# Other bounds and a place in the order for the triangular inverse of a hybrid decoder trunk

## The chip, the cores and the metric

The kernel runs on 1 core of one Trainium2 chip. The metric is device time in microseconds. An interval or a verdict compares runs of two kernels on the same chip.

## The reference

One layer on 1024 positions of width 1024, all in float32. After an RMS norm one projection feeds four groups of heads, whose outputs are normalised per head, gated and projected back:

```python
(aq, ak, av, ag, bq, bk, bv, bg, cq, ck, cv, cg, cf, d_in, dg) = _split(rms_norm(x, norm_gain) @ w_in, IN_WIDTHS)
oa = differential_attention(...)    # A: 4 heads, two softmaxes each, subtracted
ob = stick_breaking_attention(...)  # B: 8 heads, cumulative products, no softmax
oc = forgetting_attention(...)      # C: 8 heads, softmax with a forget bias
od = rwkv7_branch(...)              # D: 8 heads, a recurrence over the positions
mixed = concatenate([oa * silu(ag), ob * silu(bg), oc * silu(cg), od * silu(dg)])
return x + mixed @ w_out
```

The recurrence of group D is, for each head and position,

```python
sa = einsum('bhij,bhj->bhi', state, -kk_t)
state = state * w_t + sa[..., None] * b_t + v_t[..., None] * k_t
y_t = einsum('bhij,bhj->bhi', state, r_t)
```

## The kernel before, in words

Group D is computed in 16 chunks of 64 positions. Within a chunk the recurrence is a unit lower triangular system of 64 x 64; with 16 chunks and 8 heads there are 128 of them, one per SBUF partition. `inv_steps` inverts all of them at once on POOL (GpSimd): step r multiplies column r below the diagonal by row r (L855, `ytmp`) and adds the product to the rows below (L857, `yinv`), with 63 - r rows of r elements, cut into pieces of at most 512 elements. Steps 1 to 62 make 106 pairs of POOL instructions, each needing the one before. `inv_load` brings the matrices, `inv_store` (L861) writes the inverses to the DRAM tile `abky`, from which group D's chunks read them when all attention is done.

The attention runs as twelve jobs in a row, four of group B, four of A, four of C (the loop over `jobs`). A job projects q, k, v for its heads (`proj`, L280: 48 matmuls of 128x512 per projection, with each weight tile in two parts, `wh` in the matmul's own format and `wl` the rest), then runs `scores` (L397, L401), the group's own function of the scores, transposes of the result (L417) and the product with v (L426 to L431). The projections of job i + 1 and some gates are written behind the attention of job i, and fill TensorE between its scores. `load_w` loads half a projection's weights (`raw`, on SP's queue, L186) and has POOL split them: `wh` (L191) and `wl` (L192), two buffers each. So POOL serves the projections; in group B it also sets single columns of the scan (L472, L474), in group A it scales one softmax's exponentials (L565) ahead of the difference on DVE (L568), in group C it makes the bias tile (L613, L614) from a row `cb` that SP loads, and scales (L617). The pool that holds `yinv` and `ytmp` is closed after job 7, A3, and the pool with `cb` takes its memory.

The order of the instructions on each engine is set when the kernel is built, by a scheduler that takes, among the instructions that are ready by its own estimate, the one of the lowest priority number; each engine then runs its queue strictly in that order. The inverse is written behind each of the first eight jobs, in eight parts given by `INV_BOUNDS`, and `later(LATER)` adds 5000 to its priority number, so it goes wherever POOL would otherwise be free. `after(inst, first)` adds a dependency that the scheduler keeps in its order and that puts no semaphore into the program.

Of the kernel before, what the change touches and what calls it, by code (L numbers as in the profile page):

```python
# [19 lines left out]
P = 128  # L20
# [15 lines left out]
           dlo=7688, dg=7752)  # L36
C_ID, C_BLK, C_MS, C_MC, C_MR, C_MK, C_MN, C_I2, C_END = 0, 128, 256, 384, 512, 640, 768, 832, 896
NB = 32
INV_BOUNDS = [0, 8, 14, 20, 26, 32, 40, 50, 64]
LATER = 5000  # L40
NPT = 12
SB = 1
# [48 lines left out]
def hybrid_trunk_kernel(  # L91
# [23 lines left out]
    nc = tc.nc  # L115
# [3 lines left out]
    def pool(stack, name, bufs=1, space=None, side="left"):  # L119
        kw = {"side": side, "reuse_waits": "tile"} if space is None else {"space": space}  # L120
        return stack.enter_context(tc.tile_pool(name=name, bufs=bufs, **kw))
# [26 lines left out]
    def after(inst, first):  # L148
        tc.add_manual_dep(inst.ins, first.name if isinstance(first, mybir.InstLoadActFuncSet) else first.ins.name, mybir.DependencyInfo(
            mybir.DependencyClass.NoSync, mybir.DependencyReason.DATA), reason="order")  # L150
# [11 lines left out]

    exp_ln_tables()

# [1 line left out]
    cst = cp.tile([P, C_END], F32, name="cst")  # L166
    def vec(src, n, name, eng=nc.sync):
        t = cp.tile([P, n], F32, name=name)
# [61 lines left out]
    nc.vector.tensor_scalar(qkg[:, 0:1], qkg[:, 0:1], 0.125, None, op0=ALU.mult)  # L230
    nc.vector.tensor_scalar(qkg[:, 2:3], qkg[:, 2:3], 0.125, None, op0=ALU.mult)

# [1 line left out]
    hTh = hpool.tile([P, KT, S], F32R, name="hTh")  # L234
    hTl = hpool.tile([P, KT, S], F32R, name="hTl")

# [6 lines left out]
    with xst:  # L243
# [14 lines left out]
        for hf in range(2):  # L258
            for kt in range(KT):
# [5 lines left out]
                split = nc.scalar.activation(dh, ps, AF.Copy, scale=ng[:, kt:kt + 1])  # L265
# [1 line left out]
                    after(split, norms[ACTORD[kt]])  # L267
                nc.vector.scalar_tensor_tensor(dl, ps, ng[:, kt:kt + 1], dh.bitcast(F32), op0=ALU.mult, op1=ALU.subtract)  # L268

# [1 line left out]
    def proj(col, evac, M=P, hold=None, wts=None):  # L271
        wts = load_w(col) if wts is None else wts
        pss = [bank("pj", 2, "pj") for _ in range(2)]
        for hf in range(2):
            cs = slice(hf * HS, (hf + 1) * HS)
            n = 0
            for kt in range(KT):
                wh, wl = wts[kt // 4]
                for a, b in ((wh, hTh), (wh, hTl), (wl, hTh)):
                    mm = nc.tensor.matmul(pss[hf][:M, :], lhsT=a[:, kt % 4, :M], rhs=b[:, kt, cs], start=n == 0, stop=n == 3 * KT - 1)  # L280
                    if n == 0 and hold is not None:
                        after(mm, hold)
                    n += 1
            evac(hf, cs, pss[hf])

# [1 line left out]
    class Att:  # L287
        pass

    at = Att()  # L290
# [79 lines left out]
    def proj_gate(f, tmp):  # L370
        def evac(hf, cs, ps):
            e = tmp.tile([P, HS], F32, tag="pjt", bufs=2, name="ge")
            sigmoid(e, ps)
            nc.vector.tensor_mul(e, ps, e)
            nc.sync.dma_start(gates[f, :, cs], e)

        proj(COL["abcd"[f // 4] + "g"] + f % 4 * P, evac)
# [68 lines left out]
        nc.gpsimd.tensor_mul(y, y, gt)  # L446
        nc.sync.dma_start(mix[f * P:f * P + P, cs], y)

# [1 line left out]
    def proj_pair_b(p, pl, tmp):  # L450
        t = qk_tiles(pl)
        proj_qk(COL["bq"] + p * P, "q", t, None, tmp)
        proj_qk(COL["bk"] + p * P, "k", t, None, tmp)
        t["v"] = proj_v(COL["bv"] + p * P, pl, tmp, 2)
        return t
# [40 lines left out]
        else:  # L496
            finish(ot, f, J, blk, 64, tmp)

# [1 line left out]
    def setup_a(tmp):  # L500
        oht = tmp.tile([NB, OHW], F32, tag="oh", bufs=1, name="oht")
        nc.sync.dma_start(oht, onehot)
# [76 lines left out]
            else:  # L579
                finish(ot, p, J, ones, 128, tmp)  # L580

# [1 line left out]
    at.fbt = cp.tile([72, 1], F32, name="fbt")  # L583
    after(nc.sync.dma_start(at.fbt[64:72, :], forget_bias.rearrange("o h -> h o")), w_dma[-1])
    at.fb = at.fbt[64:72]
# [45 lines left out]
            else:  # L631
                finish(ot, 8 + p, J, blk, 64, tmp)

# [1 line left out]
    rw = Att()  # L635

    def spill(name):
# [201 lines left out]
                nc.scalar.copy(dst[64 * h:64 * h + 64, :, c2, :], src[64 * c2:64 * c2 + 64, :, h, :])  # L839
        keep(rw.rkv, 2, vt)  # L840

# [1 line left out]
    def inv_load(ip):  # L843
        rw.y = ip.tile([P, CH, CH], F32, name="yinv")
        rw.ytmp = ip.tile([P, 512], F32, name="ytmp")
        nc.sync.dma_start(rw.y.rearrange("p a b -> p (a b)"), rw.mab.rearrange("p c h t s -> (p c h) (t s)"))

    def inv_steps(r0, r1):
        y = rw.y
        for r in range(max(r0, 1), min(r1, CH - 1)):  # L850
            step = max(1, 512 // r)
            for a in range(r + 1, CH, step):
                n = min(step, CH - a)
                t = rw.ytmp[:, :n * r].rearrange("p (a b) -> p a b", b=r)
                nc.gpsimd.tensor_mul(t, y[:, a:a + n, r:r + 1].to_broadcast([P, n, r]),  # L855
                                     y[:, r:r + 1, :r].to_broadcast([P, n, r]))
                nc.gpsimd.tensor_add(y[:, a:a + n, :r], y[:, a:a + n, :r], t)  # L857

    def inv_store():
        for q in range(4):  # L860
            nc.sync.dma_start(rw.abky[:, :, 3, q].rearrange("c (h t) s -> (c h) t s", h=2), rw.y[32 * q:32 * q + 32])  # L861

# [1 line left out]
    def split_w(f, opr, wh, wl):  # L864
        raw = opr.tile([P, DM], F32, tag="raw", bufs=2, name="wraw")
        nc.sync.dma_start(raw, w_out[0, f * P:(f + 1) * P, :])
        eng = nc.vector if f in WDVE else nc.gpsimd
        if len(wh) == 1:
            nc.scalar.copy(wh[0], raw)
            eng.tensor_sub(wl[0], raw, wh[0].bitcast(F32))  # L870
        else:
            for h in range(2):
                cs = slice(h * HS, (h + 1) * HS)
                nc.scalar.copy(wh[h], raw[:, cs])
                eng.tensor_sub(wl[h], raw[:, cs], wh[h].bitcast(F32))
# [185 lines left out]
            op(y3, y3, b)  # L1061
        nc.sync.dma_start(mix[12 * P:16 * P, ts_].rearrange("(q p) t -> p q t", p=P), y3)

# [1 line left out]
    with ExitStack() as st:  # L1065
        dp0 = pool(st, "dp0", 1)
        dp = pool(st, "dp", 1)
# [12 lines left out]
    with ExitStack() as st:  # L1080
        pl = pool(st, "attw", 1)
        late_pools = st.enter_context(ExitStack())
        pp = pool(late_pools, "attp", 1)
        tmp = pool(late_pools, "attt", 1)
        side = late_pools.enter_context(ExitStack())
        inv_load(pool(side, "ip", 1))
        bounds = INV_BOUNDS
        nxt = None
        for i, (pf, af, j) in enumerate(jobs):
            cur = pf(j, pl, tmp) if nxt is None else nxt  # L1090
            at.first = None
            af(j, cur, pl, pp, tmp)
            if i == 7:
                side.close()
                at.cbp = pool(side, "cbp", 1)
            if i == 3:
                late = []
                nxt = proj_head_a(0, pl, tmp, late)
                for f in FILL[i]:
                    proj_gate(f, tmp)  # L1100
                table = exp_ln_tables()
                for g in late:
                    g(table)
            else:
                nxt = jobs[i + 1][0](jobs[i + 1][2], pl, tmp) if i + 1 < len(jobs) else None
            if i < 3:
                for f in FILL[i]:
                    proj_gate(f, tmp)
                gate_d(i, tmp)
                if i == 2:  # L1110
                    gate_d(3, tmp)
            elif i >= 7:
                for f in FILL[i]:
                    proj_gate_exp(f, at.first if i in HOLD else None)
            for f in FIN.get(i, []):
                for J in range(2):
                    finish_later(f, J, tmp)
            if i + 1 < len(bounds):
                with later(LATER):
                    inv_steps(bounds[i], bounds[i + 1])  # L1120
                    if i + 2 == len(bounds):
                        inv_store()

        hp.close()
        opr = pool(st, "opr", 1, side="right")
        rp = pool(st, "rp", 1, side="right")
        rwkv_chain_setup(rp)
        yts = {}

        def chain(c0, c1):  # L1130
            for c in range(c0, c1):
                if c % 2 == 0:
                    yts[0] = rp.tile([P, 4, P], F32, tag="yt", bufs=2, name="yt")
                chunk_state(c, rp, yts[0], chunk_local(c + 1, rp) if c + 1 < NCH else iter(()))
                if c % 2:
                    rwkv_norm(c // 2, yts[0], rp)

        for _ in chunk_local(0, rp):
            pass
        wo = {}  # L1140
        chain(0, CUT1)
        split_w_early(pl, opr, wo)
        pair = out_blocks(0, 2, wo)
        for _ in range(EARLYG):
            next(pair)
        chain(CUT1, CUT2)
        for h in at.held:
            finish(*h)
        for f in LASTF:
            for J in range(2):  # L1150
                finish_later(f, J, tmp)
        late_pools.close()
        op = pool(st, "op", 1)
        if WFIRST:
            split_w_late(op, opr, wo)
        chain(CUT2, NCH)
        if not WFIRST:
            split_w_late(op, opr, wo)
        for _ in pair:
            pass  # L1160
        for tb in range(2, 8):
            for _ in out_blocks(tb, 1, wo):
                pass
# [29 lines left out]
```

## Time and profile before

| What | Value |
|---|---|
| median of 3 runs | 1626.15 us (1625.5 to 1627.73) |
| span of the profiled execution | 1628.0 us, 23497 instructions; no other time is listed for it |
| PE (TensorE matmul) busy | 1555.1 us, 96% |
| DVE (VectorE) busy | 978.7 us, 60% |
| ACT (ScalarE) busy | 744.3 us, 46% |
| POOL (GpSimd) busy | 906.2 us, 56% |
| the inverse: L855 and L857 | 106 each, 120.6 and 127.3 us |

Shares are means over stages with different limits, so the trace is read in windows. Busy PE counts overlapping matmuls once; what the clock costs does not show in it, and stands in the column of the granted clock. Idle time counts where the engine in question sets the end. "x <- y" means that x waited for y.

### The profile page before, as it was taken

The numbers are of one execution on the slowest core, as the hardware profiler recorded it, in microseconds if no ns is written. First come the engines' busy times: TensorE is split into PE (matmuls) and PEld (weight loads), VectorE is DVE, ScalarE is ACT, GpSimd is POOL, SyncE is SP. The second block draws the span as 40 slices with busy tenths as digits, with TensorE's granted clock in tenths as the row PEclk, the third lists the DMA queues.
The fourth block names the chain that finished last, engine by engine and source line by source line (L and its number), as shares of the span: only waits on it lengthen the run. The fifth ranks groups of instructions, "written<-read, shape, count | busy, mean of one in ns | idle before, by whom it ended". The sixth has DMA issues, their size and how long they took to land.

```text
span 1628.0 us, 23497 instructions
## 1 busy us (share of the span) xinstructions
PE 1555.1 (96%) x8180; PEld 1183.9 (73%) x8180; DVE 978.7 (60%) x1739; ACT 744.3 (46%) x1601; POOL 906.2 (56%) x992
## 2 busy tenths in 40 slices
PE   6899999999989899899999999999999999999999
PEld 4777777767667676576777777777777678788887
DVE  6677763776998888466556544453456774544321
ACT  5534433443444445545556555565566654311110
POOL 3566755999999998133323356757576744300000
PEclk9999999999999999999999999999999999999999
DMA  6454567212222222622322233323227456755232
GB/s 159 102 132 102 132 163 200 59 43 71 56 62 56 78 78 57 170 52 59 98 71 72 78 91 111 97 79 111 84 84 187 120 135 165 210 140 130 82 104 65
DMA packets 259758, 168.76 MB, mean 104 GB/s; under 512 B 127948, under 2 KB 222412, under 8 KB 259512
## 3 DMA queue, kind: packets, MB, share of 16 engines
q1 hardware_dynamic: 259640, 167.26, 39.1%
q8 instruction: 65, 1.06, 0.3%
q14 instruction: 53, 0.43, 0.1%
HBM read 107.40 MB, written 49.60 MB: 96 GB/s over the span
## 4 chain that ended last, share of the span: by engine, by line
PE 64%; POOL 16%; DVE 7%; issue 6%; ACT 3%; DMA 3%; SPq 1%; POOLq 0%; DVEq 0%; ACTq 0%
PE pj L280 27%; PE pso L931 10%; POOL yinv L857 5%; POOL ytmp L855 5%; PE sc L401 5%; PE psf L968 4%; PE pt L417 3%; PE sc L397 3%; PE psn L295 3%; POOL wl L192 2%; PE po L427 2%; PE po L426 1%; POOL wh L191 1%; DMA wraw<-in_w_out_dram 1%; POOL sh L682 1%
## 5 line engine op out<-in xcount | busy, mean ns | idle before, releaser
L280 PE MATMUL pj<-hTh,wh 128*128 128x512 f32 (+1 forms) x1040 | 424.8, 409 | 14.6 <-POOL wh L191 7.2
L280 PE MATMUL pj<-hTh,wl 128*128 128x512 f32 (+1 forms) x1040 | 419.0, 407 | 12.5 <-POOL wl L192 12.1
L280 PE MATMUL pj<-hTl,wh 128*128 128x512 f32 (+1 forms) x1040 | 415.8, 400 | 0.3 <-DVE hTl L268 0.3
L280 PEld LDWEIGHTS pj<-hTh,wh 128*128 128x128 f32 (+1 forms) x1040 | 198.2, 191 | 69.7 <-issue 17.9
L280 PEld LDWEIGHTS pj<-hTh,wl 128*128 128x128 f32 (+1 forms) x1040 | 197.8, 190 | 66.6 <-POOL wl L192 17.0
L280 PEld LDWEIGHTS pj<-hTl,wh 128*128 128x128 f32 (+1 forms) x1040 | 198.0, 190 | 44.0 <-issue 5.4
L192 POOL TENSOR_TENSOR wl<-raw,wh 128x512 fp32r<-128x512 f32 (+1 forms) x130 | 185.5, 1427 | 10.5 <-PE pj L280 4.9
L191 POOL TENSOR_SCALAR wh<-raw 128x512 fp32r<-128x512 f32 (+1 forms) x130 | 100.0, 769 | 155.5 <-PE pj L280 137.7
L421 DVE TENSOR_TENSOR ptl<-pt,pth 128x512 fp32r<-128x512 f32 x240 | 126.4, 549 | 68.0 <-ACT pth L420 67.5
L420 ACT CAST pth<-pt 128x512 fp32r<-128x512 f32 x240 | 109.0, 481 | 126.8 <-PE pt L417 107.5
L475 DVE TENSOR_TENSOR_SCAN qs<-qs 128x128 f32<-128x128 f32 (+3 forms) x96 | 136.6, 1429 | 11.3 <-ACT qs L138 11.3
L553 ACT ACTIVATE Pt<-Pt,st 128x512 f32<-128x512 f32 (+2 forms) x192 | 116.8, 611 | 53.5 <-DVE st L548 52.7
L857 POOL TENSOR_TENSOR yinv<-yinv,ytmp 128x486 f32<-128x486 f32 (+44 forms) x106 | 127.3, 1201 | 4.0
L401 PE MATMUL sc<-k,ql 64*128 64x512 f32 (+3 forms) x288 | 127.6, 443 | 0.0
L855 POOL TENSOR_TENSOR ytmp<-yinv 128x486 f32<-128x486 f32 (+44 forms) x106 | 120.6, 1137 | 8.4 <-DMA raw<-in_w_in_dram 4.3
L477 DVE TENSOR_TENSOR Pt<-Pt,qs 128x128 f32<-128x128 f32 (+3 forms) x96 | 102.3, 1072 | 35.0 <-POOL qs L474 19.1
L417 PE MATMUL pt<-cst,Pt 128*128 128x128 f32 x720 | 118.0, 276 | 3.8 <-DVE Pt L477 3.8
L397 PE MATMUL sc<-k,q 128*128 128x512 f32 (+3 forms) x288 | 116.1, 403 | 2.1 <-DVE st L548 1.1
L1061 POOL TENSOR_TENSOR yc<-yc,lbg 128x512 f32<-128x512 f32 x16 | 21.2, 1325 | 150.7 <-DVE yc L1055 150.3
L417 PEld LDWEIGHTS pt<-cst,Pt 128*128 128x128 f32 x720 | 86.5, 141 | 23.3 <-issue 5.6
L401 PEld LDWEIGHTS sc<-k,ql 64*128 64x128 f32 x288 | 53.1, 185 | 68.0 <-issue 61.3
L613 POOL TENSOR_SCALAR bt<-cb,cumq 128x128 f32<-128x128 f32 (+3 forms) x64 | 52.9, 828 | 70.3 <-DVE st L548 67.8
(254 smaller groups left out, 2961.4 us busy)
## 6 DMA issues: line engine op xcount, KB each, us to landing
raw<-in_w_in_dram SPq DMA_DIRECT2D x128, 256.0 KB, 3.0
cb<-cum SPq DMA_DIRECT2D x16, 512.0 KB, 4.0
bd<-abky SPq DMA_DIRECT2D x32, 256.0 KB, 5.7
wraw<-in_w_out_dram SPq DMA_DIRECT2D x16, 512.0 KB, 4.0
om<-mix SPq DMA_DIRECT2D x32, 256.0 KB, 3.1
q<-q SPq DMA_DIRECT2D x48, 128.0 KB, 2.2
k<-kl SPq DMA_DIRECT2D x48, 128.0 KB, 2.3
gl<-gates SPq DMA_DIRECT2D x24, 256.0 KB, 3.0
```

What stands on the lines that cost most here:

```text
L191: nc.gpsimd.tensor_scalar(wh[:, :, :M], raw[:, :, :M], 1.0, 0.0, op0=ALU.mult, op1=ALU.add)
L192: nc.gpsimd.tensor_sub(wl[:, :, :M], raw[:, :, :M], wh[:, :, :M].bitcast(F32))
L280: mm = nc.tensor.matmul(pss[hf][:M, :], lhsT=a[:, kt % 4, :M], rhs=b[:, kt, cs], start=n == 0, stop=n == 3 * KT - 1)
L397: mm = nc.tensor.matmul(ps[:, :w], lhsT=t[f"q{h}"][qh][:, qs], rhs=t[f"k{h}"][:, c0:c1], start=True, stop=False)
L401: nc.tensor.matmul(ps[:, :w], lhsT=t["ql"][qh][n:n + 64, qs], rhs=t[f"k{h}"][n:n + 64, c0:c1], start=False, stop=not diag)
L417: nc.tensor.transpose(pt[:, (b - a) * P:(b - a + 1) * P], ptiles[b][kb // 4][:, kb % 4 * P:(kb % 4 + 1) * P], ident)
L421: nc.vector.tensor_sub(pl[:, :n], pt[:, :n], ph[:, :n].bitcast(F32))
L475: nc.vector.tensor_tensor_scan(q[:, :w][:, ::-1], q[:, :w][:, ::-1], q[:, :w][:, ::-1], 1.0 if after is None else after, op0=ALU.mult, op1 ...
L553: nc.scalar.activation(et[:, :w], et[:, :w], AF.Exp, scale=-1.0, bias=init, accum_out=st[:, 2 + i:3 + i])
L855: nc.gpsimd.tensor_mul(t, y[:, a:a + n, r:r + 1].to_broadcast([P, n, r]), y[:, r:r + 1, :r].to_broadcast([P, n, r]))
L857: nc.gpsimd.tensor_add(y[:, a:a + n, :r], y[:, a:a + n, :r], t)
L931: mm = nc.tensor.matmul(ps[b][half], lhsT=l, rhs=r[half], start=n == 0, stop=n == 47)
```

## The change

`INV_BOUNDS` moves the cuts: the parts written behind B0 to B3 now hold r = 1 to 11, 12 to 16, 17 to 21, 22 to 26, and those behind A0 to A3 r = 27 to 34, 35 to 41, 42 to 50, 51 to 62. Each multiplication of a part is placed behind `at.first`, the first score matmul of the job it is written behind.

```diff
-INV_BOUNDS = [0, 8, 14, 20, 26, 32, 40, 50, 64]
+INV_BOUNDS = [0, 12, 17, 22, 27, 35, 42, 51, 64]
...
-    def inv_steps(r0, r1):
+    def inv_steps(r0, r1, hold):
...
-                nc.gpsimd.tensor_mul(t, y[:, a:a + n, r:r + 1].to_broadcast([P, n, r]),
-                                     y[:, r:r + 1, :r].to_broadcast([P, n, r]))
+                mul = nc.gpsimd.tensor_mul(t, y[:, a:a + n, r:r + 1].to_broadcast([P, n, r]),
+                                           y[:, r:r + 1, :r].to_broadcast([P, n, r]))
+                after(mul, hold)
                 nc.gpsimd.tensor_add(y[:, a:a + n, :r], y[:, a:a + n, :r], t)
...
-                    inv_steps(bounds[i], bounds[i + 1])
+                    inv_steps(bounds[i], bounds[i + 1], at.first)
```

The rest of the diff turns comment lines into empty ones. The added line moves the addition from L857 to L858 and the store from L861 to L862.

The scheduler makes new orders of all engines from this. Three places show it; a row is one instruction, output tile, inputs, shape.

First, POOL in job B0, at the 45th and 46th pair of weight halves, before:

```order
L191 TENSOR_SCALAR wh<-raw 128x512
L472 MEMSET qs 128x1
L855 TENSOR_TENSOR ytmp<-yinv 128x240
L192 TENSOR_TENSOR wl<-raw,wh 128x512
L857 TENSOR_TENSOR yinv<-yinv,ytmp 128x15x16
L191 TENSOR_SCALAR wh<-raw 128x512
L855 TENSOR_TENSOR ytmp<-yinv 128x510
L192 TENSOR_TENSOR wl<-raw,wh 128x512
L474 COPY qs<-qs 128x1
L857 TENSOR_TENSOR yinv<-yinv,ytmp 128x30x17
```

The same two pairs in the change:

```order
L191 TENSOR_SCALAR wh<-raw 128x512
L192 TENSOR_TENSOR wl<-raw,wh 128x512
L472 MEMSET qs 128x1
L474 COPY qs<-qs 128x1
L191 TENSOR_SCALAR wh<-raw 128x512
L192 TENSOR_TENSOR wl<-raw,wh 128x512
L472 MEMSET qs 128x1
```

The first part (r up to 11) is done by then, and the second waits for B1, so no step of the inverse stands between the halves here. Of the 36 gaps between pairs that held steps before, from the 38th pair to the 74th, 17 hold some now.

Second, POOL in job A0, at the 80th to 82nd pair, before:

```order
L191 TENSOR_SCALAR wh<-raw 128x512
L192 TENSOR_TENSOR wl<-raw,wh 128x512
L565 TENSOR_SCALAR Pt<-Pt,st 128x512
L565 TENSOR_SCALAR Pt<-Pt,st 128x384
L191 TENSOR_SCALAR wh<-raw 128x512
```

The same place in the change:

```order
L191 TENSOR_SCALAR wh<-raw 128x512
L855 TENSOR_TENSOR ytmp<-yinv 128x495
L192 TENSOR_TENSOR wl<-raw,wh 128x512
L858 TENSOR_TENSOR yinv<-yinv,ytmp 128x15x33
L565 TENSOR_SCALAR Pt<-Pt,st 128x512 x2
L855 TENSOR_TENSOR ytmp<-yinv 128x495
L191 TENSOR_SCALAR wh<-raw 128x512
L858 TENSOR_TENSOR yinv<-yinv,ytmp 128x15x33
L192 TENSOR_TENSOR wl<-raw,wh 128x512
L855 TENSOR_TENSOR ytmp<-yinv 128x510
L858 TENSOR_TENSOR yinv<-yinv,ytmp 128x15x34
L565 TENSOR_SCALAR Pt<-Pt,st 128x128
```

Steps stand between the halves and between the scalings, through all four A jobs; the last one comes between the 96th and the 97th pair, ahead of the first `bt` of C0.

Third, SP's queue of transfers around the store, between B3 and A0 before:

```order
L186 DMA raw<-in_w_in_dram 128x4x128
L861 DMA abky<-yinv 2048x1x64 x4
L375 DMA gates<-ge 128x512
L186 DMA raw<-in_w_in_dram 128x4x128
L535 DMA tb<-skew 128x1024 x2
L342 DMA ql<-late_qk 128x512
```

In the change the store stands between A3 and C0:

```order
L493 DMA otl<-otb 128x512
L862 DMA abky<-yinv 2048x1x64 x4
L133 DMA k_8519<-kl 64x512
L133 DMA k_8520<-kl 64x512
L447 DMA mix<-y 128x512
L442 DMA gl<-gates 128x512
L186 DMA raw<-in_w_in_dram 128x4x128
L625 DMA cb<-cum 128x1024 x2
```

`ql` (raw projections of A0, kept in DRAM) no longer stands behind the store; k of C0, a weight load and the first rows `cb` do. On PE, 49 projections instead of 50 now stand ahead of C0's first score, while 37 stand ahead of A0's in both.

## Rows read from the trace of the kernel before

**Rows 1.** First score matmuls, L397: ns min/median/max, first and last start.

```profile
L397 PE MATMUL sc<-k,q x288: 220/390/797, 283.0 to 1327.4; 128*128 128x512 f32 x76, 128*128 128x128 f32 x28, 128*128 128x384 f32 x28, 128*128 128x256 f32 x12
```

**Rows 2.** Windows: us, busy PE, PEld, DVE, ACT, POOL, granted clock, DMA share, GB/s.

```profile
283.00:375.00 92.00, 88.42 (x394) 65.49 (x394) 71.45 (x75) 38.72 (x86) 89.62 (x99) 0.96 0.19 46
375.00:469.00 94.00, 85.69 (x393) 64.11 (x392) 77.42 (x84) 41.76 (x92) 89.30 (x90) 0.96 0.23 62
469.00:562.00 93.00, 85.33 (x388) 62.99 (x386) 79.77 (x86) 41.70 (x93) 90.30 (x94) 0.96 0.23 65
562.00:645.00 83.00, 79.39 (x367) 58.89 (x367) 67.67 (x76) 39.26 (x87) 80.40 (x96) 0.96 0.23 67
645.00:678.00 33.00, 25.92 (x114) 18.13 (x112) 15.82 (x24) 19.22 (x36) 5.41 (x6) 0.95 0.92 210
678.00:951.00 273.00, 272.89 (x1136) 192.59 (x1135) 160.55 (x452) 150.45 (x361) 91.64 (x109) 0.99 0.27 73
```

**Rows 3.** Timeline of PE in B0: start, us, instruction, idle before.

```profile
339.37 0.79 PE L280 MATMUL pj<-hTh,wl 128*128 128x512 f32 x1 [1.53 <-POOL wl L192]
...
340.38 0.63 PE L280 MATMUL pj<-hTl,wh 128*128 128x512 f32 x1
340.81 0.63 PE L280 MATMUL pj<-hTh,wl 128*128 128x512 f32 x1
...
342.94 0.39 PE L280 MATMUL pj<-hTl,wh 128*128 128x512 f32 x1
343.17 0.39 PE L280 MATMUL pj<-hTh,wl 128*128 128x512 f32 x1
```

**Rows 4.** Waits of PE in B, 283 to 645: us in total, times, longest.

```profile
PE pj L280 <- POOL wl L192: 10.9, 9, 2.0
PE pj L280 <- POOL wh L191: 6.8, 3, 3.2
PE pt L417 <- DVE Pt L477: 3.8, 2, 2.3
```

**Rows 5.** Groups of POOL in B: busy us, mean ns, idle before.

```profile
L857 POOL TENSOR_TENSOR yinv<-yinv,ytmp 128x486 f32<-128x486 f32 (+42 forms) x102 | 125.3, 1228 | 3.7
L855 POOL TENSOR_TENSOR ytmp<-yinv 128x504 f32<-128x504 f32 (+25 forms) x101 | 118.0, 1168 | 3.9
L192 POOL TENSOR_TENSOR wl<-raw,wh 128x512 fp32r<-128x512 f32 x36 | 56.4, 1567 | 0.1
```

**Rows 6.** Waits between B and A, 645 to 678.

```profile
ACT qn L294 <- DMA ql<-late_qk: 6.5, 1, 6.5
...
PE psn L295 <- ACT qn L294: 5.5, 1, 5.5
...
PE sc L397 <- DMA k<-kl: 0.8, 1, 0.8
```

**Rows 7.** Timeline of SP's queue, 643 to 660.

```profile
643.38 10.00 SPq L861 DMA_DIRECT2D abky<-yinv  x4
...
659.30 0.38 SPq L342 DMA_DIRECT2D ql<-late_qk  x1
```

**Rows 8.** Timeline of POOL where r = 27 begins.

```profile
414.02 1.04 POOL L855 TENSOR_TENSOR ytmp<-yinv 128x486 f32<-128x486 f32 x1
```

**Rows 9.** Windows of L855 alone: us, busy us.

```profile
414.00:643.50 229.50, 75.01 (x63) 0.97 0.22 62
```

**Rows 10.** Windows of L857 alone.

```profile
414.00:643.50 229.50, 79.00 (x63) 0.97 0.22 62
```

**Rows 11.** Window of B0's first 26 us, columns as in rows 2.

```profile
283.00:309.00 26.00, 26.00 (x121) 19.86 (x122) 18.51 (x20) 10.63 (x25) 25.37 (x31) 1.00 0.21 52
```

**Rows 12.** Groups of POOL in A: busy us, mean ns, idle before.

```profile
L192 POOL TENSOR_TENSOR wl<-raw,wh 128x512 fp32r<-128x512 f32 x25 | 33.0, 1320 | 3.4 <-PE pj L280 1.4
L565 POOL TENSOR_SCALAR Pt<-Pt,st 128x512 f32<-128x512 f32 (+3 forms) x48 | 29.5, 623 | 106.2 <-DVE st L563 74.6 <-DVE st L556 7.9 <-ACT pth L420 6.2
```

**Rows 13.** Differences on DVE in A, L568: ns min/median/max.

```profile
L568 DVE SCALAR_TENSOR_TENSOR Pt<-Pt,st x46: 335/750/1747, 682.4 to 942.5; 128x512 f32<-128x512 f32 x22, 128x128 f32<-128x128 f32 x8, 128x256 f32<-128x256 f32 x8, 128x384 f32<-128x384 f32 x8
```

## Prediction

> **What bounds the kernel now.** Job boundaries come first. Each of the twelve attention jobs issues 24 first score matmuls (L397), 288 in all, so in issue order the 1st, 25th, 49th row of L397 opens B0, B1, B2, and so on [rows 1]: B0 at 283 us, then 375, 469, 562; B's last score ends at 644; A0 opens at 678 and C0 at 951. The windows of [rows 2] are cut there. Read PE, POOL and PEclk together. Over the four A jobs, 678 to 951, PE is idle for 0.1 us of 273. In the four B jobs it is busy 88.42, 85.69, 85.33 and 79.39 us, 338.8 of 362, so 23.2 us are idle, while POOL is busy 349.6 us, 97%. The mean granted clock there is 0.96. It mixes the engine's two levels: in [rows 3] TensorE has stood idle for 1.53 us, its matmuls then come 0.43 us apart for some 3 us, which is the 1.2 GHz level, and after that 0.23 us apart, 2.4 GHz. A clock of 0.96 costs 4% of the work, (1 - 0.96) x 362 = 14.5 us. Together B loses **37.7 us** against an uninterrupted TensorE. This is an upper value, since some of the slow time is idle time too.
>
> Who makes it wait? In [rows 4] 17.7 of the 23.2 us are waits of projection matmuls for the two halves of a split weight tile, wl and wh, which POOL makes. What POOL does instead is in [rows 5]: 243.3 us of the 349.6 are the inverse (ytmp 118.0, yinv 125.3). Nothing of B needs the inverse; it only stands in the same in-order queue, as the first order place shows. So B is bound by POOL, and A by TensorE, with POOL at 91.6 of 273 us, 34%.
>
> One more stall lies between them, 645 to 678, PE 25.92 of 33 us. PE waits 5.5 us for ACT's square qn, and ACT 6.5 us for ql from DRAM [rows 6]. SP's queue shows why [rows 7]: the four stores of the finished inverse hold it for 10.00 us, and the load of ql is issued behind them at 659.30.
>
> **The change, part by part.** The 106 pairs of POOL instructions are the same, and nothing else is added: the new dependency is one of issue order, without a semaphore, so no instruction waits at run time for the score matmul itself. What changes is the place in each queue.
>
> How much moves: with the new bounds r = 1 to 26 belong to jobs B0 to B3 and r = 27 to 62 to A0 to A3. In the trace r = 27 begins at 414.02 us with a step of 18 rows of 27, 486 elements [rows 8]. From there on ytmp takes 75.01 and yinv 79.00 us [rows 9, 10]: **154.0 us** leave B for A. Of the inverse's 120.6 + 127.3 = 247.9 us, 93.9 stay in B.
>
> *B.* POOL falls from 349.6 to some 200 of 362 us. The cost that stays lies between two bounds. If a microsecond of inverse costs TensorE what it costs now, 37.7 / 243.3 = 0.155 us, the remaining 93.9 us cost 14.5. If it costs nothing, 0: in [rows 11] the first 26 us of B0 hold r up to 11, which is all of the first new part, POOL is busy 25.37 of 26 us, and PE is idle for none. The new parts in B are about that long each, and between them POOL catches up. The two rows are equally near, so I take the middle, 7.3. Gain: 37.7 - 7.3 = **30.4 us**.
>
> *A.* 154.0 us join 91.6 us. One projection (48 rows of L280) also moves from A to C in the order; TensorE is fully busy in both, so this moves 48 x 0.23 = 11 us without winning or losing any. A then has 262 us of TensorE and up to 245.6 us of POOL, 94%. By B's rate that costs 154.0 x 0.155 = 23.9 us; by A's own rows, with PE idle for nothing, 0. The instructions should also be a little cheaper there: wl takes 1320 ns in A [rows 12] against 1567 in B [rows 5]. Middle again: **+11.9 us**. What hides the rest is the projection matmuls between the scores; if POOL runs behind by more than those, this cover is gone.
>
> *Between B and A.* The store is no longer there. Gain: the 5.5 us wait and the clock of 0.95 in that stretch, (1 - 0.95) x 33 = 1.7, together **7.2 us**. Next late would be k from DRAM, now 0.8 us [rows 6]; I leave that and the smaller waits.
>
> *Between A and C.* The store now stands at the end of A3. Behind it on SP: two transfers of k for C0, the gate loads, a weight load and the first two loads of cb, which also need the memory that the inverse leaves. It holds SP for the same 10.00 us [rows 7], after SP has waited for the last step. Bounds: 0, as the projections still to run cover it, or the 7.2 us that it costs now. In A, PE is never idle, at the old place for 7.1 of 33 us, so nearer to zero: **+3 us**.
>
> Sum: -30.4 + 11.9 - 7.2 + 3 = -22.7 us. The profiled execution has a span of 1628.0 us, 1.85 above the median 1626.15; against its own time the sum gives 1605.3, against the median **1603.5 us**.
>
> **A rule to weigh.** The row first: in B, where wl is dear, DVE is busy 296.3 of 362 us; in A 160.6 of 273 [rows 2]. The Trainium skill, page "SBUF — State Buffer", section "Who interferes with whom", says that a VectorE instruction with both inputs in SBUF and a GpSimd instruction that reads SBUF exclude one another, and that the later one stands still until the first is done. By that rule the moved steps speak against the change in A: the last step of each difference (L568, both inputs in SBUF) would stand behind a step of the inverse. The trace agrees in direction only: wl is dearer where DVE is busier, but in B DVE is busy 82% and POOL 97% of the time, so most of their instructions do overlap. What that would cost is the fourth rival; the sum by it is 1648 instead of 1603.5.
>
> **The rivals.**
>
> *All of it is hidden.* POOL never falls far enough behind in either stage: 0 in B, 0 in A, 0 for the store. -37.7 - 7.2 = -44.9, 1581 us. For it: the first 26 us of B0. Against it: A's POOL would be at 94%.
>
> *Exchange.* A becomes what B was. B keeps 14.5, A pays 23.9, the store costs 7.2 in its new place: -(37.7 - 14.5) + 23.9 - 7.2 + 7.2 = +0.7, 1627 us. For it: the first parts in A are longer than those in B, and behind the first 26 us B0 does stall.
>
> *Slower: POOL stands still in front of A's scalings.* In A POOL has L565 in its queue, which scales the second softmax, and waits 106.2 us ahead of it [rows 12], mostly for DVE's st. Inverse steps that fill these waits are free; those that stand elsewhere add to them. If a share f of the waits stays, A lasts 91.6 + 154.0 + 106.2 f. That passes TensorE's 262 us from f = 0.15, and eats the other terms (30.4 + 7.2 - 3 = 34.6) from f = 0.48. At f = 0.6, A lasts 309 us, 47 more: +12.6, 1639 us. Against it: the second order place has steps between the rows of L565, right where the waits are.
>
> *Slower: A's differences are late.* The 46 rows of L568 [rows 13] each stand behind one step of 1228 ns (yinv, [rows 5]) and are on TensorE's path: 56.5 us in place of 11.9, so -22.7 - 11.9 + 56.5 = +21.9, 1648 us. That is what the rule above would make if nothing covered it. Against it: DVE idles 112 us in A, and in B, where L477 meets the same steps, TensorE waited 3.8 us for it [rows 4].
>
> *The change doesn't do what it says.* A dependency of order alone could have left POOL's queue as it was. The order shows that it did not; 1626 us.
>
> **How the numbers follow.** Forecast 0.53, all hidden 0.12, exchange 0.15, scalings 0.13, differences 0.05, nothing 0.02. A measurement of this kernel tells 0.2%, 3.3 us, from no change. Faster by more than that: forecast, all hidden and the third of the exchange in which A pays a little less than B's rate, 0.53 + 0.12 + 0.06 = 0.71. Within it: the next third and the last case, and a sliver of the scalings, 0.10. Slower: 0.19. With A's middle moved to either of its ends the forecast alone runs from 1592 to 1615. The range leaves out half of the hidden case below and the two slower ones above, 0.20 together: 1586 to 1630 us.
>
> **What would show it right or wrong.** Right: POOL near 55% over B and 85 to 95% over A; fewer than 10 us of PE idle in the four B jobs, with a clock of 0.98 or more; no wait for qn between B and A; the store some 250 us later. In A, waits for wl and wh would appear, in all some 8 us idle and a few of clock. Wrong: B's idle time stays although the inverse has gone (then DVE or ACT, not POOL, was what it waited for); or A's span grows by over 35 us, with POOL waiting for st (scalings) or PE for L568 (differences); or the first bt of C0 waits for cb and holds POOL, with weight tiles behind it.

## The result and the profile after

| | median | runs | span of the profiled execution |
|---|---|---|---|
| before | 1626.26 us | 4, 1625.5 to 1627.73 | 1628.0 us |
| changed | 1591.8 us | 4, 1588.25 to 1592.56 | 1590.5 us |

The ratio is 0.9776, 95% interval 0.9764 to 0.9788: 34.5 us faster, where 22.7 were forecast. The two profiled executions are 37.5 us apart. Line numbers behind `inv_steps` are one higher after the change: L857 is now L858, L861 is L862.

The job boundaries are again the 1st, 25th, 49th ... first score matmul. The windows of the changed kernel are cut there; columns as in [rows 2]. The first four are B0 to B3, then the stretch between B and A, all of A, then C0, C1 and C2.

```profile
283.00:367.60 84.60, 84.60 (x393) 63.79 (x394) 59.62 (x76) 38.68 (x85) 50.01 (x68) 1.00 0.21 54
367.60:449.40 81.80, 81.80 (x395) 62.63 (x394) 63.12 (x83) 41.57 (x92) 46.09 (x63) 1.00 0.25 70
449.40:529.50 80.10, 80.10 (x386) 61.17 (x385) 67.64 (x83) 41.47 (x93) 54.83 (x65) 1.00 0.28 78
529.50:609.20 79.70, 78.52 (x378) 59.34 (x377) 64.37 (x77) 39.18 (x86) 52.10 (x61) 1.00 0.23 71
609.20:636.80 27.60, 23.70 (x97) 16.65 (x95) 15.00 (x22) 17.87 (x32) 10.18 (x10) 0.88 0.43 122
636.80:898.40 261.60, 261.02 (x1094) 182.25 (x1092) 192.74 (x456) 150.75 (x360) 208.37 (x225) 1.00 0.32 83
898.40:996.00 97.60, 97.60 (x431) 72.21 (x429) 46.81 (x116) 56.81 (x126) 64.51 (x85) 1.00 0.32 97
996.00:1104.00 108.00, 108.00 (x481) 80.42 (x480) 49.54 (x120) 63.06 (x136) 70.12 (x91) 1.00 0.34 100
1104.00:1211.50 107.50, 101.04 (x439) 74.04 (x437) 53.11 (x119) 58.51 (x128) 64.64 (x82) 0.94 0.43 111
```

Beside [rows 2] three things are to be seen (C2's row of the kernel before stands below). In B, TensorE's idle time went from 23.2 to 1.2 us (326.2 less 325.02) and its clock from 0.96 to 1.00. In A, POOL went from 91.64 us of 273 to 208.37 of 261.6, 80%, and PE is still idle for only 0.6 us. And in C2 a loss has grown: 6.5 us idle, clock 0.94; before, that job had 3.4 us idle and 0.97.

```profile
1152.70:1253.00 100.30, 96.92 (x465) 72.34 (x465) 55.10 (x135) 57.90 (x131) 66.15 (x85) 0.97 0.49 125
```

The waits of PE say the same. In the changed kernel, first B (283 to 609), then the stretch between B and A, then A:

```profile
PE pj L280 <- POOL wh L191: 0.9, 1, 0.9
PE sc L397 <- issue: 0.4, 1, 0.4
PE pj L280 <- POOL wl L192: 0.3, 1, 0.3
...
PE po L426 <- DVE ot L437: 3.8, 1, 3.8
...
PE sc L397 <- DVE st L548: 0.4, 1, 0.4
PE po L430 <- DVE ptl L421: 0.2, 1, 0.2
```

The 17.7 us for wl and wh of [rows 4] are 1.2. The wait for qn [rows 6] is gone; in its place comes a shorter one, for the head output ot. In A no wait for wl or wh has appeared.

Where the 37.5 us of the two executions went, stage by stage, is worked out from the scores that bound the stages (before: B0 283.0, end of B's last score 644.0, A0 677.8, C0 951.1, end 1628.0; after: 282.9, 609.2, 636.8, 898.4, 1590.5). The order moves 11 us of one projection from A to C; the table counts them in A in both kernels:

| stage | before | after | difference | forecast |
|---|---|---|---|---|
| B0 to B's last score | 361.0 | 326.3 | -34.7 | -30.4 |
| from there to A0 | 33.8 | 27.6 | -6.2 | -7.2 |
| A, with those 11 us | 273.3 | 272.6 | -0.7 | +11.9 |
| C and the rest, without them | 676.9 | 681.1 | +4.2 | +3 (store) |

### The profile page after: what moved, and what is told of

It reads as the page before. It is cut to its first block, busy times and chain, and to the rows that moved or that the text cites. A ratio compares the mean times of both kernels' runs of the same rounds, so it can differ in the third digit from the quotient of the medians.

```text
span 1590.5 us, 23481 instructions
## 1 busy us (share of the span) xinstructions
PE 1540.5 (97%) x8180; PEld 1177.2 (74%) x8180; DVE 975.6 (61%) x1739; ACT 747.0 (47%) x1601; POOL 884.6 (56%) x992
## 4 chain that ended last, share of the span: by engine, by line
PE 80%; DVE 6%; POOL 5%; ACT 3%; issue 3%; DMA 2%; SPq 1%; POOLq 0%; ACTq 0%; DVEq 0%
PE pj L280 37%; PE pso L932 10%; PE sc L401 6%; PE psf L969 5%; PE pt L417 5%; PE sc L397 4%; PE psn L295 3%; PE po L427 2%; PE po L426 2%; POOL wl L192 1%; DMA wraw<-in_w_out_dram 1%; PE pvt L358 1%; POOL yinv L858 1%; PE po L430 1%; POOL wh L191 1%
## 5 line engine op out<-in xcount | busy, mean ns | idle before, releaser
L280 PEld LDWEIGHTS pj<-hTh,wh 128*128 128x128 f32 (+1 forms) x1040 | 195.7, 188 | 58.3 <-issue 17.7
L192 POOL TENSOR_TENSOR wl<-raw,wh 128x512 fp32r<-128x512 f32 (+1 forms) x130 | 190.1, 1462 | 10.9 <-PE pj L280 5.8
L191 POOL TENSOR_SCALAR wh<-raw 128x512 fp32r<-128x512 f32 (+1 forms) x130 | 96.4, 741 | 117.7 <-PE pj L280 104.9
L475 DVE TENSOR_TENSOR_SCAN qs<-qs 128x128 f32<-128x128 f32 (+3 forms) x96 | 116.3, 1217 | 19.9 <-ACT qs L138 19.7
L858 POOL TENSOR_TENSOR yinv<-yinv,ytmp 128x486 f32<-128x486 f32 (+44 forms) x106 | 118.4, 1117 | 4.3
L397 PE MATMUL sc<-k,q 128*128 128x512 f32 (+3 forms) x288 | 114.7, 398 | 0.8 <-DVE st L548 0.4
L855 POOL TENSOR_TENSOR ytmp<-yinv 128x486 f32<-128x486 f32 (+44 forms) x106 | 105.8, 998 | 3.9
L932 PE MATMUL pso<-wol,omh 128*128 128x512 f32 x224 | 89.1, 398 | 0.0
```

The costliest lines, as they stand in the source:

```text
L191: nc.gpsimd.tensor_scalar(wh[:, :, :M], raw[:, :, :M], 1.0, 0.0, op0=ALU.mult, op1=ALU.add)
L192: nc.gpsimd.tensor_sub(wl[:, :, :M], raw[:, :, :M], wh[:, :, :M].bitcast(F32))
L397: mm = nc.tensor.matmul(ps[:, :w], lhsT=t[f"q{h}"][qh][:, qs], rhs=t[f"k{h}"][:, c0:c1], start=True, stop=False)
L475: nc.vector.tensor_tensor_scan(q[:, :w][:, ::-1], q[:, :w][:, ::-1], q[:, :w][:, ::-1], 1.0 if after is None else after, op0=ALU.mult, op1 ...
L932: mm = nc.tensor.matmul(ps[b][half], lhsT=l, rhs=r[half], start=n == 0, stop=n == 47)
```

## The experiments

### Which half of the change is it?

The kernel before with the new bounds and no dependency:

```diff
-INV_BOUNDS = [0, 8, 14, 20, 26, 32, 40, 50, 64]
+INV_BOUNDS = [0, 12, 17, 22, 27, 35, 42, 51, 64]
```

> New bounds, no place in the order. The built POOL queue is the same as before, row for row, as the scheduler still packs the inverse into B. Theory (the steps in POOL's queue of B make TensorE wait): as before, 1626 us within 5, POOL 97% in B. Rival (the new cuts themselves help, or any new order is luckier): some 1600 us.

Measured: 1628.84 us over 10 runs, beside 1628.35 for the kernel before; ratio 1.0004 (0.9995 to 1.0014). The order of POOL's instructions is row for row that of before.

The change with the old bounds, so the dependency alone:

```diff
-INV_BOUNDS = [0, 12, 17, 22, 27, 35, 42, 51, 64]
+INV_BOUNDS = [0, 8, 14, 20, 26, 32, 40, 50, 64]
```

> Old bounds, with the place in the order: r = 1 to 25 behind B0 to B3 and 26 to 62 behind A0 to A3, nearly the same shares as the change. Theory: as the change, 1592 us within 4, PE idle in B under 4 us. Rival (the cuts were chosen to fit and matter): 1600 to 1615 us.

Measured: 1589.88 us, ratio 0.9767 (0.9748 to 0.9787). Its row for 283 to 609:

```profile
283.00:609.00 326.00, 323.88 (x1540) 245.58 (x1539) 247.79 (x317) 159.80 (x354) 196.71 (x252) 1.00 0.25 67
```

What follows: the new numbers do nothing by themselves. Without a dependency the parts keep one another's order and flow together into the first places that POOL has free; it is `after` that makes a bound a bound. Given the dependency, either set of bounds gives the whole effect.

### Is it the inverse in B that TensorE lost time to?

Two kernels with the dependency. In the first, the loop leaves out all of the inverse's steps but the last, so the inverse is not computed:

```diff
-        for r in range(max(r0, 1), min(r1, CH - 1)):
+        for r in range(max(r0, CH - 2), min(r1, CH - 1)):
```

In the second, all steps stand behind B0 to B3:

```diff
-INV_BOUNDS = [0, 12, 17, 22, 27, 35, 42, 51, 64]
+INV_BOUNDS = [0, 19, 31, 43, 64, 64, 64, 64, 64]
```

> The change without steps r = 1 to 61 of the inverse (left out, so the inverse is not computed); load, store and the last step stay. Theory (A covers all of it and B's short bursts cost about 1 us): no more than 5 us below the change, 1587 to 1592 us. Rival (A pays about 12 us for its 126 us of inverse, as forecast): 1575 to 1580 us.

> The place in the order kept, but all 62 steps behind B0 to B3 (bounds 0, 19, 31, 43, 64), spread more evenly over B than before. Theory (POOL over-full in B): PE idle in B about 20 us and a clock of 0.96 to 0.97 again, 1615 to 1630 us. Rival (being held back to its job is what helps, not leaving B): 1600 us or less.

Measured: without the steps 1586.57 us, ratio 0.9742 (0.9725 to 0.9758); with all of them in B 1627.79 us over 10 runs, ratio 0.9995 (0.9985 to 1.0004). The window from 283 to 609 of the one, then of the other, with two of the other's waits of PE from 283 to 700:

```profile
283.00:609.00 326.00, 326.00 (x1555) 249.30 (x1556) 221.99 (x317) 159.85 (x353) 97.99 (x171) 1.00 0.24 68
```

```profile
283.00:609.00 326.00, 309.18 (x1419) 231.53 (x1418) 273.66 (x288) 149.10 (x329) 304.57 (x326) 0.97 0.23 62
...
PE pj L280 <- POOL wh L191: 13.1, 7, 3.8
PE pj L280 <- POOL wl L192: 6.6, 6, 2.2
```

What follows: with POOL busy 97.99 us, TensorE loses nothing; with 304.57, 93%, it is idle for 16.8 us and waits for wl and wh as before, held back or not. So the gain is from steps that leave B. (In the second kernel the store is still issued between B and A, at 659; what its place is worth is tried below.) The changed kernel, at 1591.8 us and 1590.3 in a later series, is 4 to 5 us above the kernel without steps: what is left of the inverse's cost is about that, as far as times of different chips can be set side by side.

### How much can A take?

All steps behind A0 to A3, and, after that, a smaller shift:

```diff
-INV_BOUNDS = [0, 12, 17, 22, 27, 35, 42, 51, 64]
+INV_BOUNDS = [0, 1, 1, 1, 1, 20, 32, 46, 64]
```

> All 62 steps behind A0 to A3. POOL in A: 208 us now plus about 75 more, 283 us against 262 us of TensorE. Theory (a stage pays once POOL has more to do than TensorE): A grows to 285 us or more with PE idle, and some 20 to 40 us slower than the change, 1612 to 1635 us; B loses nothing. Rival (A's filler covers any amount): within 5 us of the change.

```diff
-INV_BOUNDS = [0, 12, 17, 22, 27, 35, 42, 51, 64]
+INV_BOUNDS = [0, 7, 12, 16, 20, 30, 38, 47, 64]
```

> Bounds 0, 7, 12, 16, 20, 30, 38, 47, 64: about 30 us more of the inverse move from B to A; POOL in A about 235 of 262 us, 90%. Theory: still under TensorE's time, so within 4 us of the change, 1588 to 1596 us. Rival (loss grows with POOL's share, as B's did): 5 to 12 us slower than the change.

Measured: 1661.28 us, ratio 1.0209 (1.0187 to 1.0232), and 1619.28 us over 7 runs, ratio 0.9936 (0.9914 to 0.9958). Both expectations missed. Yet A itself lost almost nothing in either: with the smaller shift PE is idle for 0.8 us of A's 264.1, at a clock of 0.99. With all steps in A, the last of them run on into C0 and end at 965; in that kernel, the window of A, then the first job of C:

```profile
635.00:896.50 261.50, 260.81 (x1091) 182.44 (x1089) 190.60 (x447) 144.73 (x350) 227.44 (x237) 1.00 0.28 73
...
896.50:1059.20 162.70, 94.15 (x377) 66.08 (x377) 47.39 (x123) 55.12 (x124) 114.10 (x150) 0.76 0.26 67
```

Its waits of PE from 635 to 1060, and the timeline of ACT and the store's rows of the same kernel:

```profile
PE pj L280 <- ACT gg L382: 59.7, 1, 59.7
...
980.55 1.07 ACT L382 COPY gg<-pj 128x512 f32<-128x512 f32 x2 [57.71 <-DMA abky<-yinv]
...
L862 SPq DMA_DIRECT2D abky<-yinv x4: 654/2810/3502, 965.3 to 971.8; - x4
```

One wait is most of the loss: in C0 PE is idle for 68.6 us (162.70 less 94.15), 59.7 of them here, and the clock around it is 0.76. The gate projection of group C is evacuated by ACT into gg, a tile of the pool `cbp`, and this pool is made of the memory that `side.close()` takes back from the inverse: ACT's copy waits 57.71 us for the store of yinv, and the projection's PSUM bank with it. In the kernel with the smaller shift the same wait is 13.8 us; C0 begins at 900, the inverse ends at 916. Its waits of PE from 636 to 1010, ACT and SP's queue:

```profile
PE pj L280 <- ACT gg L382: 13.8, 1, 13.8
...
931.68 1.07 ACT L382 COPY gg<-pj 128x512 f32<-128x512 f32 x2 [12.51 <-DMA abky<-yinv]
...
916.26 9.98 SPq L862 DMA_DIRECT2D abky<-yinv  x4
```

Here ACT's copy comes 5.4 us behind the point at which the store leaves SP (926.24), and in the kernel with all steps in A by about as much. In the changed kernel the store leaves SP at 874.87 (864.85 and 10.02) and the copy comes at 892.5, so some 12 us are in hand, an estimate. The kernel with the old bounds and the dependency, whose last step begins at 877.9 instead of 863.2, already has ACT wait 1.2 us for this store.

That reading was tested: the smaller shift again, with gg and gx in the temporaries' pool.

```diff
-            g = at.cbp.tile([P, HS], F32, tag="gg", bufs=2, name="gg")
+            g = tmp.tile([P, HS], F32, tag="pjt", bufs=2, name="gg")
...
-            e = at.cbp.tile([P, HS], F32, tag="ge", bufs=2, name="gx")
+            e = tmp.tile([P, HS], F32, tag="gx", bufs=2, name="gx")
```

> The kernel that moves still more of the inverse into A (1619.3 us), with the gate projection's two tiles gg and ge of the pool cbp put into the temporaries' pool, so that they no longer need the memory that the inverse leaves (cb still does). Since the tiles are free, the order lets these matmuls come earlier. Theory (the 27 us at the start of C0 were lost because ACT could not evacuate the gate projection before the inverse's memory was free): the wait of pj for gg (13.8 us) is gone, C0 loses under 5 us, and the kernel takes 1592 to 1602 us. Rival (POOL has too much to do at the end of A, whatever the memory): PE waits for wl, st or a scaled tile instead, and the time stays above 1610 us.

Measured: 1596.85 us, ratio 0.9813 (0.9791 to 0.9836), 22 us below the same bounds without it. The inverse now ends later, at 920, and it no longer matters. The edit also lets the order bring these projections earlier: the first copy of gg is at 884.6, ahead of the inverse's end. C0's window, and all waits of PE from 636 to 1010:

```profile
908.50:1012.60 104.10, 102.30 (x447) 74.61 (x445) 47.26 (x116) 58.62 (x128) 76.37 (x104) 1.00 0.49 127
...
PE sc L397 <- DVE st L548: 1.0, 2, 0.7
PE pj L280 <- POOL wl L192: 0.8, 1, 0.8
PE psn L295 <- ACT qn L238: 0.6, 1, 0.6
PE pt L417 <- POOL Pt L617: 0.4, 1, 0.4
```

What follows: POOL at 227.44 of 261.5 us, 87%, in the kernel with all steps in A, costs A 0.7 us of idle time at most (here it is 236.12 of 272.6, with 1.0 us idle); what limits the shift is when the inverse gives its memory back. The changed kernel, at 1590.3 in the same series, stays ahead of this one; where those 6.5 us lie was not settled.

### Was it the store?

The kernel before, with the four stores placed behind A3's first score and nothing else moved:

```diff
-    def inv_store():
+    def inv_store(hold):
         for q in range(4):
-            nc.sync.dma_start(rw.abky[...], rw.y[32 * q:32 * q + 32])
+            d = nc.sync.dma_start(rw.abky[...], rw.y[32 * q:32 * q + 32])
+            after(d, hold)
...
-                        inv_store()
+                        inv_store(at.first)
```

> The kernel before, with only the store of the inverse moved behind A3's first score; the steps stay in B. Theory: the wait of 5.5 us between B and A and its slow clock go, 6 to 8 us faster than before, 1618 to 1621 us; PE idle in B stays 23 us. Rival (the store was most of the gain): 1600 us or less. Other rival (ql was late for another reason): 1626 us.

Measured: 1625.58 us over 10 runs, which lie between 1617.7 and 1632.2; ratio 0.9986 (0.9968 to 1.0004). The 6 to 8 us are not shown. In its profile (span 1621.5) the wait for qn is gone and A0 comes at 666.5, C0 at 944.4 in place of 951.1, while the waits for wl and wh in B stay (283 to 700):

```profile
PE pj L280 <- POOL wl L192: 12.0, 9, 2.0
PE pj L280 <- POOL wh L191: 6.4, 3, 3.2
```

So the store did cause the wait between B and A; what it is worth in time alone stays open within these runs' spread. That it was most of the gain is excluded.

### The loss that grew in C2

In the changed kernel's timelines, DVE, then PE, then POOL at 1188 us:

```profile
1188.24 6.70 DVE L958 COPY rkv<-cst 128x256 f32<-128x256 f32 x2
1194.86 0.54 DVE L421 TENSOR_TENSOR ptl<-pt,pth 128x384 fp32r<-128x384 f32 x1
...
1195.46 0.69 PE L427 MATMUL po<-ptl,vs 128*128 128x384 f32 x1 [5.66 <-DVE ptl L421]
...
1188.19 1.81 POOL L952 MEMSET bd<- 128x2048 f32 x1
1189.93 0.95 POOL L956 MEMSET bdm<- 128x1024 f32 x1
1190.83 1.81 POOL L952 MEMSET bd<- 128x2048 f32 x1
1192.57 0.95 POOL L956 MEMSET bdm<- 128x1024 f32 x1
1193.49 1.29 POOL L386 TENSOR_TENSOR gx<-gg,gx 128x512 f32<-128x512 f32 x1
```

Two copies of 128x256 by DVE take 6.70 us together while POOL fills tiles with zeros. In the kernel before, where they are on L957, they took 0.29 and 1.98 us:

```profile
L957 DVE COPY rkv<-cst x2: 294/1134/1975, 1226.1 to 1226.3; 128x256 f32<-128x256 f32 x2
```

Behind them on DVE stands ptl, behind ptl a matmul that waits 5.66 us. Two kernels move the copies off DVE, the first to POOL, the second to ACT; the first was run in two series, the second time beside the change itself.

```diff
-            nc.vector.tensor_copy(t[:, 3], ...)
+            nc.gpsimd.tensor_copy(t[:, 3], ...)
...
+            nc.scalar.copy(t[:, 3], ...)
```

> The change, with the two copies of the identity into rkv (L958) on POOL behind its memsets instead of on DVE. In the change they took 1.3 and 5.4 us on DVE while POOL cleared bd and bdm, and PE stood idle for 5.7 us behind them. Theory: that wait and the slow clock behind it go, 5 to 10 us faster than the change, 1582 to 1587 us. Rival (TensorE would have been short of work there anyway): within 2 us of the change.

> The change itself once more, so that the two places for the copies are compared with it beside the same runs of the kernel before. Expected 1591.8 us within 1.5, and in the profile again two copies of the chunk recurrence (L958) on DVE that take several us while POOL runs the four memsets (L952, L956) between C1 and C2.

> The change with the two copies L958 on POOL, behind its own memsets, as in the earlier run, now beside the change itself. Theory (DVE's copies are held while POOL's memsets run, and ptl and the product behind them wait): 3 to 6 us faster than the change, C2 about 102 us long instead of 107.5. Rival (the difference between the two earlier series was one of chips and batches): within 1.5 us of the change.

> The change with the two copies L958 on ACT instead of DVE. Theory (only DVE's copies stand behind POOL's memsets; ACT's don't): the copies take under 1 us each, the wait of the product for ptl between C1 and C2 is gone, and the kernel is 3 to 6 us faster than the change. Rival (the copies wait for whatever engine shares SBUF with POOL): a copy on ACT takes several us too, and C2 stays at 107 us.

| | median | ratio to before | C2 |
|---|---|---|---|
| the change, again | 1590.3 us | 0.9765 (0.9747 to 0.9784) | 106.0 us |
| copies on POOL, first series | 1587.35 us | 0.9752 (0.9733 to 0.977) | 101.9 us |
| copies on POOL, again | 1587.3 us | 0.975 (0.9732 to 0.9767) | 101.8 us |
| copies on ACT | 1591.54 us | 0.978 (0.9758 to 0.9802) | 103.2 us |

The groups of the copies, in the change run again, on ACT and on POOL:

```profile
L958 DVE COPY rkv<-cst x2: 1342/3390/5439, 1186.4 to 1191.8; 128x256 f32<-128x256 f32 x2
```

```profile
L958 ACT COPY rkv<-cst x2: 417/417/417, 1188.4 to 1188.8; 128x256 f32<-128x256 f32 x2
```

```profile
L958 POOL COPY rkv<-cst x2: 403/494/584, 1189.4 to 1192.3; 128x256 f32<-128x256 f32 x2
```

What follows: the place is shown, since the same copy at the same moment takes 0.42 us on ACT, and C2 is 3 to 4 us shorter in both versions. The worth is less sure. On POOL the kernel is 3.0 us faster than the change beside it, at the low end of what was expected then and below the 5 to 10 us expected first, with intervals that still overlap. On ACT nothing of it arrives, against the expectation: its last job and the tail, 1205.8 to the end at 1588.9, take 383.1 us, against 379.8 in the change run again; why was not tried. The version with the copies on POOL has the lowest median of all that compute the whole, in both series, and is a likely gain over the change, not a certain one.

## Why the prediction was right, and where it was off

The time fell inside the range and the mechanism was the one forecast: steps that B doesn't need stood in POOL's queue ahead of the weight tiles. The gain was 1.5 times the forecast. The prediction gives 1592 us for A at its lower end, and 1591.8 were measured; that the two agree so closely is in part luck, since the other terms missed by up to 4.3 us in both directions. Two of its sums of chances are slightly off (a third of 0.15 is 0.05, not 0.06, and what the range leaves out is 0.24, not 0.20); the forecast does not hang on them. By the steps of the sum, as the two profiled executions show them:

- **B, -30.4: measured -34.7.** The residual was sized as the middle of 0 and 14.5. Of its two rows the one that held was [rows 11], the 26 us in which POOL was full and TensorE lost nothing: 1.2 us idle at clock 1.00 are left. POOL's share was forecast near 55% and is 203.0 of 326.2 us, 62%, in a shorter B.
- **A, +11.9: measured -0.7.** This is the term that failed, and most of the miss. The upper end took B's rate, 0.155 us per microsecond of inverse, to a stage where POOL is less full. A's clock gives some 1.8 of the difference, an estimate (A0 ran at 0.97 for 60.4 us before and at 1.00 after), so the steps cost A about 1 us. Two numbers under the term were off. The moved steps were priced at 154.0 us; the same 63 and 63 instructions take 131.7 after (rows below), and some of them run ahead of A0. With the projection that left, POOL is at 80% and not at 94. And the run with all steps in A shows 87% with 0.7 us lost, while at 93 and 97% in B TensorE stood idle for 16.8 of 326 and 23.2 of 362 us. B and A differ in more than POOL's share, so no threshold follows; but the price is not proportional to the work, and a middle of two ends was the wrong form for it.
- **Between B and A, -7.2: measured -6.2.** The wait for qn went with the store, as forecast; what is late next was not k but ot, 3.8 us, and the clock there is 0.88 instead of 0.95.
- **The store, +3: nothing found.** It is issued at 864.85 and holds SP for 10.02 us [rows 7], 221 us later rather than some 250. POOL's first bt of C0 does wait 3.76 us for cb, one of the signs listed for a failure, and C0 has no idle time of PE all the same: the cover held. What the prediction did not name beside cb is gg, which needs the same memory and is what waits when the inverse ends later. The +4.2 in C and behind it goes with the copies: with them on POOL, C and the rest take 687.1 us (896.9 to 1584.0), 676.1 without the 11, against 676.9 before.
- **Forecast signs in A.** Waits for wl and wh, some 8 us idle and a few of clock: none came.

The windows of L855 and of L858 alone in the changed kernel, 622 to 865, that stand against [rows 9] and [rows 10]:

```profile
622.00:865.00 243.00, 60.94 (x63) 0.99 0.27 72
...
622.00:865.00 243.00, 70.73 (x63) 0.99 0.27 72
```

The steps that stayed in B are no cheaper (92.6 us against 93.9). Two other runs tell that it is the stage and not the step. In the kernel with all steps in B the steps from r = 27 on take 148.5 us; in the one with all steps in A the steps up to r = 26, from 621 to 776, take 82.4, for L855 and then L858:

```profile
621.00:775.90 154.90, 39.15 (x43) 1.00 0.29 78
...
621.00:776.00 155.00, 43.20 (x43) 1.00 0.29 78
```

What in the stage does it was not tried. The prediction had the direction, from wl, and left it out of the sum.

**The rivals.** "All of it is hidden" came as near as the forecast: 1581 against 1591.8 measured, where the forecast said 1603.5, and it had 0.12. The loss "exchange" is out, since A lost next to nothing. "Scalings" is answered by POOL's groups in A, after:

```profile
L192 POOL TENSOR_TENSOR wl<-raw,wh 128x512 fp32r<-128x512 f32 x23 | 31.3, 1361 | 0.6 <-PE pj L280 0.5
L565 POOL TENSOR_SCALAR Pt<-Pt,st 128x512 f32<-128x512 f32 (+3 forms) x48 | 29.6, 626 | 42.2 <-DVE st L563 21.9 <-ACT q L322 13.1 <-ACT sq L238 5.6
```

The idle time ahead of L565 fell from 106.2 us [rows 12] to 42.2: the steps fill the waits. 42.2 of 106.2 is f = 0.40, past the 0.15 at which the prediction had A grow: by its formula A would last 288 us. But with POOL busy for 208.4 us instead of 245.6 the two add up to 250.6, and fit A's 261.6. "Differences" had its mechanism and not its price. L568 in A (47 rows), in the changed kernel and then in the kernel without the steps:

```profile
L568 DVE SCALAR_TENSOR_TENSOR Pt<-Pt,st 128x512 f32<-128x512 f32 (+3 forms) x47 | 51.1, 1112 | 3.4 <-POOL Pt L565 1.4
```

```profile
L568 DVE SCALAR_TENSOR_TENSOR Pt<-Pt,st 128x512 f32<-128x512 f32 (+3 forms) x47 | 30.2, 669 | 2.5 <-POOL Pt L565 0.8
```

The differences did become dearer by 20.9 us, and no matmul waited for them in A; DVE had the room, at 192.74 of 261.6 us. The rule of the Trainium skill weighed ahead of the result (page "SBUF — State Buffer", section "Who interferes with whom") fits in kind: L568 has both inputs in SBUF, and its median is 1180 ns where the steps run beside it, 745 to 750 in three kernels where they don't. In B the same shows from the other side: with fewer steps beside them DVE's 321 instructions take 254.8 us, where they took 296.3 [rows 2]. How much of B's gain came by way of DVE was not separated; TensorE's waits there were for POOL's tiles.

## What to carry to other kernels

Work that nobody waits for belongs behind the stage in which its engine is full, and a priority alone does not put it there: a part needs a dependency in the order to stay in its place. Before such work is moved further, look for what waits for its memory, not only for its result; in the kernel with all steps in A that wait, 59.7 us in one row, was the limit, and no share of busy time showed it. Price a queue by the stage's own slack, not by a rate from a stage in which the queue was full.

## What the runs showed of the hardware

- DVE's copies L958 took 5.4 and 1.3 us while POOL ran four memsets and a product: the first from 1188.24 until the fourth memset was over (1193.52), the second until the product was (1194.78). One of them took 0.29 us on DVE in the kernel before, and both take 0.42 us on ACT in the same place. The Trainium skill, page "SBUF — State Buffer", section "Who interferes with whom", says that a DVE copy in a two-port mode and a GpSimd instruction exclude one another. The trace fits that, though no row names the copy's mode, and shows more: one copy was held past four GpSimd instructions in a row. In the kernel before, the copy of 1.98 us got in behind one memset, of 1.95 us.
- With TensorE idle for 1.2 us in 326, its mean granted clock in B is 1.00, the 2.4 GHz level; in the 162.7 us around the single wait of 59.7 us it averages 0.76, a mix with the 1.2 GHz level.
